# Conditioning rows loaded two weight tiles ahead of their sums, a row every six weight tiles, and the square of a relu on ScalarE

## The chip, the cores and the metric

The kernel runs on one core of a Trainium2 chip. A core has a matrix engine (TensorE, PE in the profile), three engines for elementwise work (VectorE or DVE, ScalarE or ACT, GpSimd or POOL) and an engine, SyncE (SP), that here only issues DMA transfers. Each engine runs its own instructions in the order in which they were put, and waits on semaphores for the others. The metric is the device time of one execution in microseconds, and lower is better.

## The reference

Two blocks of transformer layers run one after the other on 256 tokens of width 1024, all in fp32. The first block has two layers with three kinds of attention and an MLP with a squared relu. The second has two layers whose norms and outputs are conditioned on a vector: the `adaln` product gives a shift, a scale and a gate, for the tokens and for a context of 256 more.

```
def hybrid_layer(x, norm_mix, w_in, ..., w_o, norm_mlp, w_up, w_down, pos):
...
    return x + jnp.square(jax.nn.relu(h @ w_up)) @ w_down

def adaln(cond, w, b):
    m = jnp.matmul(jax.nn.silu(cond), w) + b
    return jnp.split(m, 3, axis=-1)

def modulated_norm(x, g, shift, scale):
    return rms_norm(x, g) * (1 + scale) + shift

def second_block(x, c, ctx, c_ctx, ...):
    for layer in range(DEPTH):
        shift, scale, gate = adaln(c, w_ada[layer], b_ada[layer])
        c_shift, c_scale, c_gate = adaln(c_ctx, w_ada[layer], b_ada[layer])
...
        x = x + gate[:, None] * jnp.matmul(y, w_out[layer])
        if need_ctx:
            x_ctx = x_ctx + c_gate * jnp.matmul(y_ctx, w_out[layer])
```

The `adaln` products do not depend on `x`, so the kernel may compute them at any time before block 2 uses them.

## The kernel before

The activations lie with the features on the partitions, in eight chunks of 128 x 256 tokens (`x0` to `x7`, which the order of the instructions below calls `x_92` to `x_99`). All matrix products are made of weight tiles of 128 x 1024 fp32 (512 KB). `weights()` loads one from HBM on SP's queue into one of six `raw` buffers (L284), lets ScalarE round it to a high part `hi` (L293) and VectorE subtract that from it to get the low part `lo` (L294; a few on POOL). There are three buffers each for `hi` and `lo`. TensorE then makes three matmuls for each product, `hi`·`h`, `hi`·`h`'s low part and `lo`·`h` (L336 to L338), 24 for a weight tile. The activations are split in the same way (`h` on L497 and L498, `ul`, `el` and others on L278).

The order on each engine is not written out. The kernel is a program of tiles, and a scheduler sets the order of the instructions from the order of the calls, its own model of the time and the free buffers.

After each attention, `wo` tiles project out, and each of the eight chunks of `x` is updated (L757 in block 1, L1168 for block 2's `wo2`); the squares of the new `x` are summed for the next norm: ScalarE squares (L421), POOL adds (L425), and TensorE makes the mean with an extra matmul (`ps_n`, L430). Then comes the MLP: 16 pairs of `wu` tiles, each ending in a relu on ScalarE (L774), its square (L775) and the split, and `wd` tiles, whose sums update `x` (L789, L790).

The conditioning product is made by VectorE. `wada` is laid out so that 48 tiles of 128 x 1024, here called rows, hold what 128 outputs of `adaln` need. A dot (L859) multiplies such a tile with the conditioning vector `crow` of the tokens or of the context and sums along it; the last eight rows need one dot only, so that there are 88. A generator (`Ada.rows`) goes one step forward on each fourth weight tile (`Ada.call`, at the end of `weights()`). `until(24)`, ahead of block 2, and `until(48)`, ahead of the norm of its second layer, run what is left of the rows that they need.

Of the kernel before, what the change touches and what calls it, by code (L numbers as in the profile page):

```python
# [12 lines left out]
AF = mybir.ActivationFunctionType  # L13
# [199 lines left out]
class _K:  # L213
# [4 lines left out]
    def __init__(self, tc, ctx, ins):  # L218
        self.tc, self.nc, self.ins = tc, tc.nc, ins
        pool = lambda n, **kw: ctx.enter_context(tc.tile_pool(name=n, bufs=1, **kw))  # L220
        self.res, self.wp, self.up, self.tp = pool("res"), pool("w"), pool("u"), pool("t")
        self.ps = pool("ps", space=PSUM)
        self.log_table, self.tanhs = None, []

        self.pending, self.rate = [], 1

        self.flows, self.tail = [], None

        self.rows = None
# [259 lines left out]
def block1(k, x, first, layers=(0, 1), fill=None):  # L489
    nc, ins = k.nc, k.ins  # L490
    g1 = k.g1

    def gx(c, gi):

        g = g1[:, gi * 8 + c:gi * 8 + c + 1]
        hi, lo = k.pair("h")
        nc.scalar.activation(hi, x[c], AF.Copy, scale=g)  # L497
        nc.vector.scalar_tensor_tensor(lo, x[c], g, hi, op0=ALU.mult, op1=ALU.subtract)  # L498
        return hi, lo
# [7 lines left out]
    for l in layers:  # L507
# [253 lines left out]
        for hf in range(2):  # L761
            u = []
            for b in range(8 * hf, 8 * hf + 8):
                p = k.psum()
                for f in range(2):
                    k.fm(p[:, f * T:(f + 1) * T], k.weights(ins["wu"][l, 2 * b + f]), 0, h)
                if rs2 is None:
                    rs2 = k.rstd(acc)
                    nc.vector.tensor_mul(rs2, rs2, rs2)
                    acc = k.acc()  # L770
                if fill:
                    fill(l, 1)
                r, uh, ul = k.t2("r"), k.u("uh", F32R, "v"), k.u("ul", F32R, "v")
                nc.scalar.activation(r, p, AF.Relu)  # L774
                nc.vector.tensor_mul(r, r, r)  # L775
                k.split(uh, ul, r)
                for f in range(2):
                    s = slice(f * T, (f + 1) * T)
                    u.append((uh[:, s], ul[:, s]))
            if hf:  # L780
                h = []
                if l == layers[-1]:
                    acc2 = k.acc()
            for c in range(NCH):
                p = k.psum()
                for q in range(2):
                    k.fm(p[:, :T], k.weights(ins["wd"][l, 2 * hf + q, c]), 0, u[8 * q:8 * q + 8], q == 0, q == 1)
                t = k.t1("dn")
                nc.vector.tensor_mul(t, p[:, :T], rs2)  # L789
                nc.vector.tensor_add(x[c], x[c], t)  # L790
                if fill:
                    fill(l, 1)
                if hf:
                    if l != layers[-1]:
                        h.append(gx(c, 2 * l + 2))
                    acc.add(c, x[c])
                    if l == layers[-1]:
                        acc2.add(c, x[c], g1[:, 32 + c:33 + c])
# [31 lines left out]
class Ada:  # L830

    EVERY = 4

    def __init__(self, k, cd):
        self.k, nc, ins = k, k.nc, k.ins
        sc, e = (k.res.tile([P, 2, NCH], F32, name=n) for n in ("sc", "sce"))
# [14 lines left out]
    def rows(self):  # L853
        k, nc = self.k, self.k.nc
        for l, i in ADA_ORDER:
            raw = k.raw(k.ins["wada"][l, i])
            for j in range(1 if (l, i // 8) == (1, 2) else 2):
                junk = k.tp.tile([P, D], mybir.dt.bfloat16, name="dot", tag="dot", bufs=1)
                nc.vector.tensor_tensor_reduce(out=junk, in0=raw, in1=self.c[:, j], scale=1.0, scalar=self.b[:, l, i:i + 1],  # L859
                                               op0=ALU.mult, op1=ALU.add, accum_out=k.ada[:, l, i, j:j + 1])  # L860
                yield
            self.done += 1
            if i == 15:
                v = k.ada[:, l, 8:16, :]
                nc.vector.tensor_scalar(v, v, 1.0, None, op0=ALU.add)
                nc.vector.tensor_tensor(v, v, k.g2[:, 8 * l:8 * l + 8, None].to_broadcast([P, 8, 2]), op=ALU.mult)

    def call(self):
        self.calls += 1
        if self.calls % self.EVERY == 0:  # L870
            next(self.steps, None)

    def until(self, n):
# [538 lines left out]
def _program(tc, ins, out, stop=7):  # L1412
    nc = tc.nc
    with ExitStack() as ctx:
# [68 lines left out]
        if stop & 3:  # L1483
            finish = block1(k, x, first, [l for l in range(2) if stop >> l & 1], fill if stop & 4 else None)
# [27 lines left out]
```

## Time and profile before

| | |
|---|---|
| time, median of 3 runs | 1436.06 us (1435.83 to 1436.11) |
| the profiled execution | 1436.98 us, of which the span of the trace is 1435.2 us |
| granted TensorE clock | 0.998 of full speed |
| TensorE (PE) busy | 1406.4 us, 98% |
| VectorE (DVE) busy | 1146.4 us, 80% |
| ScalarE (ACT) busy | 771.4 us, 54% |
| GpSimd (POOL) busy | 101.4 us, 7% |
| DMA engines busy | 49.3% for the weight queue |

Busy times are of one profiled execution. A matmul's duration overlaps with the next one's, so a busy TensorE is not a TensorE at its peak. In the timelines a row has the start in us from the beginning of the span, the duration, the engine, the line, the operation and its tiles, and in brackets how long the engine stood idle before it and what it waited for. Block 1 lasts until about 940 us.

### The profile page before, as it was taken

The page shows a single profiled execution, that of the slowest core. Times are in us where ns is not written, and L with a number is a line of the kernel's source. Part 1 is how long each engine was busy: PE and PEld are TensorE (multiplying, and loading weights), DVE is VectorE, ACT ScalarE, POOL GpSimd, SP SyncE. Part 2 cuts the span into 40 slices and gives each one's busy share as a digit, 9 for nine tenths or more (in the row PEclk, how much of TensorE's full clock was granted, in tenths as well). Part 3 has the DMA queues.
Part 4 walks back from the last instruction along what each step waited for, and adds up shares of the span by engine and source line. Part 5 has one row for each costly group of instructions (what it writes and reads, how often), then busy time and mean ns, then how long its engine had stood idle before and what let it go on. Part 6 is the DMA issues. An engine that isn't in the chain of part 4 may idle for free. (4 is left out here: it accounts for less than half of the span.)

```text
span 1435.2 us, 26253 instructions
## 1 busy us (share of the span) xinstructions
PE 1406.4 (98%) x10324; PEld 1281.4 (89%) x10324; DVE 1146.4 (80%) x2044; ACT 771.4 (54%) x1395; POOL 101.4 (7%) x84
## 2 busy tenths in 40 slices
PE   8999999999999999999999999989999999999999
PEld 7989999999999888899998999977677888987798
DVE  6887778998789887777888778788769979986776
ACT  5455665553455445556465455556653344656664
POOL 2000000100012200000011200310001002100000
PEclk9999999999999999999999999999999999999999
DMA  7734655665766563556575657642132128421223
GB/s 273 229 115 155 189 174 183 217 207 193 234 209 201 188 206 116 159 178 191 168 224 196 213 199 234 206 147 96 45 108 100 58 103 293 169 89 45 74 89 103
DMA packets 74279, 235.97 MB, mean 164 GB/s; under 512 B 9163, under 2 KB 11820, under 8 KB 74028
## 3 DMA queue, kind: packets, MB, share of 16 engines
q1 hardware_dynamic: 72284, 232.70, 49.3%
q8 instruction: 81, 1.33, 0.4%
q10 hardware_dynamic: 1872, 1.59, 0.3%
q14 instruction: 42, 0.34, 0.1%
HBM read 230.59 MB, written 3.68 MB: 163 GB/s over the span
## 5 line engine op out<-in xcount | busy, mean ns | idle before, releaser
L293 ACT CAST hi<-raw 128x1024 fp32r<-128x1024 f32 (+2 forms) x378 | 380.1, 1009 | 364.7 <-PE ps_mm L337 221.9
L294 DVE TENSOR_TENSOR lo<-raw,hi 128x1024 fp32r<-128x1024 f32 (+2 forms) x367 | 432.6, 1181 | 139.8 <-ACT hi L293 137.4
L336 PE MATMUL ps_mm<-h,hi 128*128 128x256 f32 (+1 forms) x1712 | 521.1, 305 | 2.2 <-ACT hi L293 0.8
L338 PE MATMUL ps_mm<-h,lo 128*128 128x256 f32 (+1 forms) x1712 | 511.5, 299 | 3.9 <-DVE lo L294 3.9
L337 PE MATMUL ps_mm<-h,hi 128*128 128x256 f32 (+1 forms) x1712 | 509.9, 298 | 1.2 <-DVE h L498 1.0
L336 PEld LDWEIGHTS ps_mm<-h,hi 128*128 128x128 f32 x1712 | 327.4, 191 | 29.9 <-issue 18.5
L338 PEld LDWEIGHTS ps_mm<-h,lo 128*128 128x128 f32 x1712 | 327.5, 191 | 16.5 <-DVE lo L294 5.2
L337 PEld LDWEIGHTS ps_mm<-h,hi 128*128 128x128 f32 x1712 | 327.6, 191 | 12.7 <-DVE h L498 2.8
L336 PE MATMUL ps_mm<-uh,hi 128*128 128x256 f32 x512 | 145.2, 284 | 0.0
L337 PE MATMUL ps_mm<-ul,hi 128*128 128x256 f32 x512 | 145.1, 283 | 0.1
L338 PE MATMUL ps_mm<-uh,lo 128*128 128x256 f32 x512 | 144.6, 283 | 0.0
L859 DVE CUSTOM_DVE_ANT_0 dot<-raw,crow,bada 128x1024 bf16<-128x1024 f32 x88 | 116.7, 1327 | 12.2 <-DMA raw<-wada 11.8
L425 POOL TENSOR_TENSOR acc<-acc,sq 128x256 f32<-128x256 f32 x54 | 52.3, 973 | 710.9 <-ACT sq L421 710.2
L336 PEld LDWEIGHTS ps_mm<-uh,hi 128*128 128x128 f32 x512 | 98.1, 192 | 2.6 <-issue 2.1
L337 PEld LDWEIGHTS ps_mm<-ul,hi 128*128 128x128 f32 x512 | 98.2, 192 | 1.0 <-DVE ul L278 0.5
L338 PEld LDWEIGHTS ps_mm<-uh,lo 128*128 128x128 f32 x512 | 98.1, 192 | 0.0
L336 PE MATMUL ps_mm<-hi,h 128*128 128x384 f32 (+1 forms) x192 | 62.6, 326 | 0.0
L337 PE MATMUL ps_mm<-lo,h 128*128 128x384 f32 (+1 forms) x192 | 61.3, 319 | 0.2 <-DVE lo L294 0.2
L338 PE MATMUL ps_mm<-hi,h 128*128 128x384 f32 (+1 forms) x192 | 61.2, 319 | 0.0
L336 PE MATMUL ps_mm<-y,hi 128*128 128x256 f32 x192 | 55.0, 288 | 0.0
L338 PE MATMUL ps_mm<-y,lo 128*128 128x256 f32 x192 | 54.9, 287 | 0.0
L337 PE MATMUL ps_mm<-y,hi 128*128 128x256 f32 x192 | 54.6, 285 | 0.0
(331 smaller groups left out, 2351.6 us busy)
## 6 DMA issues: line engine op xcount, KB each, us to landing
raw<-wu SPq DMA_DIRECT2D x64, 512.0 KB, 4.2
raw<-wd SPq DMA_DIRECT2D x64, 512.0 KB, 3.9
raw<-wada SPq DMA_DIRECT2D x48, 512.0 KB, 3.5
raw<-wg SPq DMA_DIRECT2D x48, 512.0 KB, 3.9
raw<-wo SPq DMA_DIRECT2D x48, 512.0 KB, 4.0
raw<-wqk SPq DMA_DIRECT2D x46, 512.0 KB, 4.5
raw<-w2e SPq DMA_DIRECT2D x32, 512.0 KB, 3.5
raw<-wv SPq DMA_DIRECT2D x32, 384.0 KB, 3.5
```

Of the source, the lines that this page charges most:

```text
L293: self.nc.scalar.copy(hi[:, s], raw[:, s])
L294: (self.nc.gpsimd if pool else self.nc.vector).tensor_sub(lo[:, s], raw[:, s], hi[:, s])
L336: mm(out, wh, xh, start=start, stop=False)
L337: mm(out, wh, xl, start=False, stop=False)
L338: mm(out, wl, xh, start=False, stop=stop)
L425: nc.gpsimd.tensor_add(self.sum, self.sum, sq)
L859: nc.vector.tensor_tensor_reduce(out=junk, in0=raw, in1=self.c[:, j], scale=1.0, scalar=self.b[:, l, i:i + 1], op0=ALU.mult, op1=ALU.add, ...
```

## The change

The generator now yields twice between a row's load and its first dot, and once after each dot as before. `call` steps it forward on four weight tiles of each six. The square of the relu is an activation on ScalarE in place of a product on VectorE.

```
                 nc.scalar.activation(r, p, AF.Relu)
-                nc.vector.tensor_mul(r, r, r)
+                nc.scalar.activation(r, r, AF.Square)
                 k.split(uh, ul, r)
...
-    EVERY = 4
-
...
         for l, i in ADA_ORDER:
             raw = k.raw(k.ins["wada"][l, i])
+            yield
+            yield
             for j in range(1 if (l, i // 8) == (1, 2) else 2):
...
     def call(self):
+
         self.calls += 1
-        if self.calls % self.EVERY == 0:
+        if self.calls % 6 < 4:
             next(self.steps, None)
```

Three places show how the instructions move. The first is VectorE at the last updates of `x` ahead of the MLP of block 1's first layer (`x_97` to `x_99` are the chunks 5 to 7, `h` the low part of the MLP's input, L859 a dot and the reading of its sum). Before:

```order
L498 SCALAR_TENSOR_TENSOR h<-x_97,g_90,h 128x256
L757 TENSOR_TENSOR x_98<-ps_mm,x_98 128x256
L294 TENSOR_TENSOR lo<-raw,hi 128x1024
L498 SCALAR_TENSOR_TENSOR h<-x_98,g_90,h 128x256
L757 TENSOR_TENSOR x_99<-ps_mm,x_99 128x256
L294 TENSOR_TENSOR lo<-raw,hi 128x1024
L498 SCALAR_TENSOR_TENSOR h<-x_99,g_90,h 128x256
L294 TENSOR_TENSOR lo<-raw,hi 128x1024
```

and in the changed kernel:

```order
L498 SCALAR_TENSOR_TENSOR h<-x_97,g_90,h 128x256
L859 ISA dot,adaT<-raw,crow,bada 128x1024
L859 ISA adaT 128x1
L757 TENSOR_TENSOR x_98<-ps_mm,x_98 128x256
L294 TENSOR_TENSOR lo<-raw,hi 128x1024
L498 SCALAR_TENSOR_TENSOR h<-x_98,g_90,h 128x256
L757 TENSOR_TENSOR x_99<-ps_mm,x_99 128x256
L859 ISA dot,adaT<-raw,crow,bada 128x1024
L859 ISA adaT 128x1
L498 SCALAR_TENSOR_TENSOR h<-x_99,g_90,h 128x256
L294 TENSOR_TENSOR lo<-raw,hi 128x1024 x3
```

Two dots now stand between the updates, and one of the `lo` tiles has moved behind the last `h`.

The second is VectorE at the end of block 2's first output projection, with the updates of `x_98` and `x_99` (chunks 6 and 7; L1168 is L1169 in the changed kernel) and the norm behind them (`nt`). Before:

```order
L859 ISA dot,adaT<-raw,crow,bada 128x1024
L859 ISA adaT 128x1
L1168 SCALAR_TENSOR_TENSOR x_98<-ps_mm,adaT,x_98 128x256
L859 ISA dot,adaT<-raw,crow,bada 128x1024
L859 ISA adaT 128x1
L859 ISA dot,adaT<-raw,crow,bada 128x1024
L859 ISA adaT 128x1
L1168 SCALAR_TENSOR_TENSOR x_99<-ps_mm,adaT,x_99 128x256
L294 TENSOR_TENSOR lo<-raw,hi 128x1024 x3
L376 SCALAR_TENSOR_TENSOR nt<-ps_n,rstd 128x256
L377 SCALAR_TENSOR_TENSOR nt<-nt,rstd 128x256
```

and in the changed kernel, from the update of chunk 5:

```order
L1169 SCALAR_TENSOR_TENSOR x_97<-ps_mm,adaT,x_97 128x256
L294 TENSOR_TENSOR lo<-raw,hi 128x1024
L1169 SCALAR_TENSOR_TENSOR x_98<-ps_mm,adaT,x_98 128x256
L294 TENSOR_TENSOR lo<-raw,hi 128x1024
L1169 SCALAR_TENSOR_TENSOR x_99<-ps_mm,adaT,x_99 128x256
L294 TENSOR_TENSOR lo<-raw,hi 128x1024
L376 SCALAR_TENSOR_TENSOR nt<-ps_n,rstd 128x256
L377 SCALAR_TENSOR_TENSOR nt<-nt,rstd 128x256
```

The dots are gone, and a `lo` tile follows each update.

The third is VectorE at the end of block 1's first MLP and the start of the second layer: the last `x` (`x_99`), its `h`, the first projection's `sh` and the norm `nt`. Before:

```order
L790 TENSOR_TENSOR x_99<-x_99,dn 128x256
L294 TENSOR_TENSOR lo<-raw,hi 128x1024
L498 SCALAR_TENSOR_TENSOR h<-x_99,g_90,h 128x256
L294 TENSOR_TENSOR lo<-raw,hi 128x1024
L542 STREAM_SHUFFLE sh<-ps_mm 128x512
L294 TENSOR_TENSOR lo<-raw,hi 128x1024
L859 ISA dot,adaT<-raw,crow,bada 128x1024
L859 ISA adaT 128x1
L859 ISA dot,adaT<-raw,crow,bada 128x1024
L859 ISA adaT 128x1
L294 TENSOR_TENSOR lo<-raw,hi 128x1024
L376 SCALAR_TENSOR_TENSOR nt<-ps_n,rstd 128x256
```

and in the changed kernel:

```order
L859 ISA dot,adaT<-raw,crow,bada 128x1024
L859 ISA adaT 128x1
L789 TENSOR_TENSOR dn<-ps_mm,rstd 128x256
L294 TENSOR_TENSOR lo<-raw,hi 128x1024
L790 TENSOR_TENSOR x_99<-x_99,dn 128x256
L859 ISA dot,adaT<-raw,crow,bada 128x1024
L859 ISA adaT 128x1
L498 SCALAR_TENSOR_TENSOR h<-x_99,g_90,h 128x256
L294 TENSOR_TENSOR lo<-raw,hi 128x1024
L542 STREAM_SHUFFLE sh<-ps_mm 128x512
L294 TENSOR_TENSOR lo<-raw,hi 128x1024 x2
L376 SCALAR_TENSOR_TENSOR nt<-ps_n,rstd 128x256
```

The two dots that stood ahead of the norm now stand around the last update of `x`, and one `lo` has moved ahead of that update.

## Rows read from the trace of the kernel before

**Rows 1.** The page, part 1: busy us of each engine, share of the span, instructions.
```profile
PE 1406.4 (98%) x10324; PEld 1281.4 (89%) x10324; DVE 1146.4 (80%) x2044; ACT 771.4 (54%) x1395; POOL 101.4 (7%) x84
```

**Rows 2.** Table of windows: busy time of each engine in two stretches.
```profile
core 0: us, PE busy (x) PEld busy (x) DVE busy (x) ACT busy (x) POOL busy (x), PEclk, DMA share, GB/s
1184.00:1212.00 28.00, 25.17 (x193) 24.28 (x193) 27.00 (x38) 13.97 (x21) 6.74 (x6) 0.96 0.85 291
...
300.00:460.00 160.00, 159.95 (x1276) 154.07 (x1275) 132.21 (x192) 77.56 (x98) 12.22 (x9) 1.00 0.64 208
```

**Rows 3.** The page, part 5: the dots; busy, mean ns, idle before, releaser.
```profile
L859 DVE CUSTOM_DVE_ANT_0 dot<-raw,crow,bada 128x1024 bf16<-128x1024 f32 x88 | 116.7, 1327 | 12.2 <-DMA raw<-wada 11.8
```

**Rows 4.** Table of waits: us in total, times, longest.
```profile
DVE dot L859 <- DMA raw<-wada: 11.8, 14, 2.1
```

**Rows 5.** Table of windows for the tile dot alone: first window.
```profile
0.00:920.00 920.00, 91.09 (x70) 1.00 0.60 194
```

**Rows 6.** Timeline of TensorE at 1205: start, duration, operation, [idle before, releaser].
```profile
1205.51 0.28 PE L338 MATMUL ps_mm<-y,lo 128*128 128x256 f32 x1
...
1207.79 0.70 PE L430 MATMUL ps_n<-acc,im 128*128 128x256 f32 x2 [2.00 <-POOL acc L425]
...
1209.79 1.22 PE L430 MATMUL ps_n<-sq,im 128*128 128x256 f32 x2 [0.83 <-ACT sq L421]
...
1212.94 0.34 PE L336 MATMUL ps_mm<-y,hi 128*128 128x256 f32 x1
```

**Rows 7.** Timeline of VectorE at 1200 to 1210.
```profile
1200.52 1.76 DVE L859 CUSTOM_DVE_ANT_0 dot<-raw,crow,bada 128x1024 bf16<-128x1024 f32 x1
...
1208.75 0.47 DVE L1168 SCALAR_TENSOR_TENSOR x<-ps_mm,adaT,x 128x256 f32<-128x256 f32 x1
1209.15 1.21 DVE L294 TENSOR_TENSOR lo<-raw,hi 128x1024 fp32r<-128x1024 f32 x1
```

**Rows 8.** Timeline of POOL (GpSimd) at 1200.
```profile
1200.11 1.07 POOL L425 TENSOR_TENSOR acc<-acc,sq 128x256 f32<-128x256 f32 x1 [2.15 <-ACT sq L421]
```

**Rows 9.** Timeline of TensorE: eight instructions behind a wait.
```profile
473.78 0.39 PE L337 MATMUL ps_mm<-h,hi 128*128 128x256 f32 x1 [0.33 <-DVE h L498]
...
487.38 0.27 PE L434 MATMUL ps_n<-im,acc 128*128 128x2 f32 x1 [0.73 <-DVE nt L376]
...
491.91 0.35 PE L336 MATMUL ps_mm<-h,hi 128*128 128x256 f32 x1 [0.62 <-DVE ntok L377]
...
531.54 0.48 PE L594 MATMUL ps_s<-qk 64*128 64x256 f32 x1 [0.76 <-DVE mn L599]
...
535.75 0.48 PE L594 MATMUL ps_s<-qk 64*128 64x256 f32 x1 [0.62 <-DVE mn L599]
...
957.98 1.12 PE L1050 MATMUL ps_n<-qsq,bo 128*128 128x512 f32 x2 [1.95 <-DVE qn L376]
...
961.98 1.12 PE L1050 MATMUL ps_n<-qsq,bo 128*128 128x512 f32 x2 [1.70 <-DVE qr L1054]
...
1080.31 0.50 PE L337 MATMUL ps_s<-el,fwh 128*128 128x512 f32 x1 [1.38 <-DVE el L278]
```

**Rows 10.** Timeline of VectorE at the places ahead of such waits.
```profile
276.49 0.47 DVE L498 SCALAR_TENSOR_TENSOR h<-x,g,h 128x256 fp32r<-128x256 f32 x1
...
483.24 1.29 DVE L859 CUSTOM_DVE_ANT_0 dot<-raw,crow,bada 128x1024 bf16<-128x1024 f32 x1 [1.09 <-DMA raw<-wada]
...
528.58 1.28 DVE L859 CUSTOM_DVE_ANT_0 dot<-raw,crow,bada 128x1024 bf16<-128x1024 f32 x1 [2.10 <-DMA raw<-wada]
...
954.78 1.27 DVE L859 CUSTOM_DVE_ANT_0 dot<-raw,crow,bada 128x1024 bf16<-128x1024 f32 x1
...
1075.02 1.28 DVE L859 CUSTOM_DVE_ANT_0 dot<-raw,crow,bada 128x1024 bf16<-128x1024 f32 x1 [1.88 <-DMA raw<-wada]
```

**Rows 11.** The tile r: relu and square; min/median/max ns.
```profile
L774 ACT ACTIVATE r<-ps_mm x32: 578/590/597, 281.7 to 889.9; 128x512 f32<-128x512 f32 x32
L775 DVE TENSOR_TENSOR r<-r x32: 676/682/689, 285.4 to 891.1; 128x512 f32<-128x512 f32 x32
```

More of the change, by code (lines that the diff above doesn't have):

```diff
@@ L774, in block1 @@
                 nc.scalar.activation(r, p, AF.Relu)
-                nc.vector.tensor_mul(r, r, r)
+                nc.scalar.activation(r, r, AF.Square)
                 k.split(uh, ul, r)
@@ L830 @@
 class Ada:
-    EVERY = 4
     def __init__(self, k, cd):
@@ L856, in rows @@
             raw = k.raw(k.ins["wada"][l, i])
+            yield
+            yield
             for j in range(1 if (l, i // 8) == (1, 2) else 2):
@@ L869, in call @@
         self.calls += 1
-        if self.calls % self.EVERY == 0:
+        if self.calls % 6 < 4:
             next(self.steps, None)
```

## The prediction

> **What bounds the kernel now.** I read the engines' busy time first. TensorE is busy for 1406.4 of 1435.2 us [rows 1], so all its idle time together is 28.8 us. No change in who waits for whom can bring much more than that, and no edit here takes a matmul away. So I looked for the stretches where TensorE loses time. The table of windows shows two kinds. From 300 to 460 us, in the middle of an MLP, TensorE is busy for 159.95 of 160 us (1276 matmuls, 0.125 us each), and VectorE for 132.21: there VectorE has 27.8 us to spare, and what it does costs nothing. From 1184 to 1212 us, at block 2's first output projection, it is the other way round: VectorE 27.00 of 28, TensorE 25.17 [rows 2]. The question is therefore where VectorE's order puts work ahead of something that TensorE waits for.
>
> The conditioning rows' dots are 88 instructions of 1327 ns, 116.7 us in all [rows 3]. VectorE also stands idle ahead of 14 of them, 11.8 us together, until the row's `wada` load has landed [rows 4]; since its instructions run in order, all that follows waits too. 70 of the 88 start before 920 us [rows 5], the other 18 in block 2. By the text of the change a row goes from eight weight tiles to six (to four and a half where it has one dot): 40 × 6 + 8 × 4.5 = 276 weight tiles for all rows, where it was 40 × 8 + 8 × 4 = 352. In the order of the changed kernel the last dot stands ahead of the end of block 1's last MLP, and block 2 has none. So each dot is either gone from where it was, or new somewhere earlier, and I priced the places one by one.
>
> **What the change takes away.**
>
> *The burst at 1188 to 1209 us.* The last eight dots stand between the eight updates of `x` (L1168). TensorE ends a matmul at 1205.51 + 0.28, waits 2.00 for POOL's sum of squares, then 0.83 for the last square, and is back at its usual work at 1212.94 [rows 6]. Between 1205.51 and 1212.94 lie 15 matmuls of 0.125 us and four passes of the mean (L430), which I put at 0.22 each (0.70 is shown for two that overlap): 1.9 + 0.9 = 2.8 of 7.4 us. So 4.6 are lost. The last `x` is updated at 1208.75, right behind two dots, and the `lo` of the next weight tile follows at 1209.15 [rows 7]; only then can the last square and the third matmul of each sum come. Without dots, the last update can follow its projection's last matmul at 1205.8, its square about 1 us later, and the new order has two `lo`s in hand by then. I take 4.5 of the 4.6, with 3 to 4.7 as bounds.
>
> The dot at 1200.52 took 1.76 us where one elsewhere takes 1.27 [rows 7, 10]; POOL's add of 1.07 us had begun at 1200.11 [rows 8] and ends where 0.5 us of the dot are explained. On this the Trainium skill, "SBUF — State Buffer" (SBUF: two separate sides), says that a VectorE instruction with two SBUF inputs and a GpSimd one share a port pair under an exclusive lock, so that the later one stands still until the earlier ends. The trace agrees (1.76 against 1.27). By that rule a dot beside an add would cost 0.5 us more wherever it is put.
>
> *Start of block 2, 954 to 962 us.* Two dots stand in the chain of the first key norm: one at 954.78, ahead of `qn` at about 957.5, the other ahead of `qr`. TensorE waits 1.95 and 1.70 there [rows 9, 10]. Without the first, `qn` comes 1.2 earlier; the second wait goes wholly. That is 2.9 at most. The scheduler has also reordered this attention, so I take 2.5 (0.5 to 2.9).
>
> *1075 to 1080 us.* VectorE waits 1.88 for `wada` and then makes two dots, ahead of the `lo` half of the hyena input (`el`); TensorE waits 1.38 for it [rows 9, 10]. The 1.88 + 2 × 1.28 = 4.4 us of delay vanish: 1.4 (1.0 to 1.5).
>
> *Layer 1 of block 1, 483 to 536 us.* At 483.24 a dot has waited 1.09 for its row, and a second one follows, ahead of a `lo` and the norm: TensorE waits 0.73 at 487.38, and 0.62 at 491.91. At 528.58 a dot has waited 2.10, ahead of the attention's scores (0.76 at 531.54), and another delays the second group (0.62 at 535.75) [rows 9, 10]. In the new order the first pair is gone, the pair at 528 is still there but without the wait for its load, and the last dot is gone. I take 0.7 + 0.5 + 0.6 + 0.6 = 2.4 (1 to 2.7).
>
> *The other six dots of block 2* (18 less the burst's eight, less two each at 954 and 1075) lie between waits of other causes; by the smallest wait above, 0.6, for one or two of them: 1.0 (0 to 2).
>
> Sum of the gains: 4.5 + 2.5 + 1.4 + 2.4 + 1.0 = 11.8.
>
> **What it adds.** 18 more dots now run before 920 us. Most fall in MLPs, where the spare 27.8 us of a 160 us stretch hide them [rows 2]. Were that cover gone, each would cost 1.28. Five places have none.
>
> *Start of both MLPs.* In layer 0 `h` of `x7` is made at 276.49 and `lo` tiles stand between the updates [rows 10]. Now two dots stand there, and one `lo` moves behind the last `h`. One more instruction of 1.2 in the chain makes `h` late by 1.2, and the displaced `lo` (needed at once by the next weight tile) ends some 0.5 late on top: 1.7. In layer 1 one dot stood there and now three do, with the same shift: 1.7. Together 3.4 (1.5 to 5; with POOL's adds beside each dot it is nearer the upper end).
>
> *End of layer 0's MLP.* TensorE waits 0.33 at 473.78 for the last `h` [rows 9]. Two dots now stand ahead of it; in the new order TensorE has 17 matmuls of a later tile (2.1 us) to make meanwhile, against 2.5 us of dots and a `lo` moved ahead: 0.6 (0 to 1.5).
>
> *The first 80 us and block 1's attention.* Two and about eight more dots; in the first, SP's queue also waits for the conditioning vector ahead of a weight load. Where I compared the orders, none stands right ahead of a norm or a score at which the old had none: 0.5 each (0 to 1, 0 to 1.5).
>
> *Loads.* A row holds one of six raw buffers for five tiles of six instead of four of eight. The weights lost a buffer of lead then too, and the table of waits names no wait for a load of `wu` or `wd`. Nothing.
>
> *The square on ScalarE.* r·r took 682 ns on VectorE; the relu of the same shape takes 590 on ScalarE [rows 11], so I price Square at 590 too (bounds 0.4 to 0.7). In 160 us of MLP ScalarE is busy for 77.56 [rows 2]; the 32 squares add 32 × 0.59 = 19 us over both layers, and VectorE is spared 32 × 0.682 = 21.8. TensorE is full on either side and the chain relu, square, cast, `ul` ends 0.1 us sooner. Nothing either way (−1 to +1).
> The Trainium skill, "ScalarE: Activation LUTs" (Rules for kernel authors), advises against this: simple functions such as `mul` belong on VectorE, not ScalarE. The trace differs for this fp32 shape: 682 on VectorE against 590 on ScalarE. By the rule the edit would lose time (rival 4); by the rows it is neutral.
>
> Sum of the costs: 3.4 + 0.6 + 0.5 + 0.5 = 5.0. Net 6.8 us. The profiled execution took 1436.98 us beside a median of 1436.06; its 1435.2 us of span become 1428.4, and the median 1436.1 − 6.8 = 1429.3.
>
> **The rivals.** What a measurement can tell from no change is 0.2%, 2.9 us: faster is below 1433.2, slower above 1438.9.
> 1. *Only the burst pays.* The rest of block 2 waits for something else next (the scheduler moved matmuls too), and layer 1 keeps its waits, while the costs come: 1436.1 − 4.5 − 1.4 + 5.0 = 1435.2, or 1432.7 if half of the costs do. For it: the waits of 0.6 to 0.8 have other instructions close behind. Against: two of them have an idle VectorE right ahead, waiting for `wada` [rows 10].
> 2. *The earlier dots cost more than the late ones did (slower).* The mechanism is one dot, 1.28 us (1.76 beside POOL), ahead of a norm, score or `h` in block 1. 18 of them come to 23 us. It decides from 11.8 + 2.9 = 14.7 us, 11 or 12 of the 18 uncovered: 1440. For it: five already are, by the order. Against: the cover in the MLPs [rows 2].
> 3. *Gain without the costs.* The `h` chain at the MLP starts has slack that the rows hide: 1436.1 − 11.8 = 1424.3.
> 4. *ScalarE's square binds.* Each half of an MLP ends its up projections with a square that may queue behind a relu and a cast of its own shape and so come 2 × 0.59 later than VectorE's did, with the sum for `wd` waiting; four halves, 4.7 us: 1429.3 + 4.7 = 1434. For it: nothing in the rows. Against: ScalarE's idle half [rows 2]. The page "ScalarE: Activation LUTs" of the Trainium skill, cited above, stands on this rival's side.
> 5. *The rows are not done in time* and block 2 makes a burst again: no change, 1436. Against: the order has no dot there.
>
> **How the numbers follow.** Forecast 0.56, its own range 1425.5 to 1432.5; rival 1 0.17; rival 2 0.08; rival 3 0.10; rival 4 0.05; rival 5 0.04. Faster are the forecast, rival 3 and half of rival 1 (0.74, with a little of rival 4, 0.76); same are the other half of rival 1, most of rival 4 and rival 5 (0.16); slower is 0.08. To leave no more than 2 in 10 out, the range reaches from just under rival 3 to rival 1's upper end: 1423 to 1435.5.
>
> **What the new profile would show.** VectorE's busy share from 1184 to 1212 falls from 27.00 by about 12 us and TensorE's waits of 2.00 and 0.83 are gone (step 1). No dot starts after about 890 us. VectorE's wait for `wada` falls from 11.8 to near nothing. Waits of 0.6 and more at 487, 531, 535, 958, 962 and 1080 are gone or below 0.3. TensorE's wait for `h` of `x7` at the MLP starts grows from some 0.2 to over 1. No wait names the Square. I would be wrong if the MLP starts cost over 3 us each, if the qk norm of block 2 waits for ScalarE instead, or if weight loads come late beside the rows.

## The result and the profile after

The changed kernel took 1447.1 us (median of 4 runs, 1444.92 to 1449.52), the kernel before 1436.09 (1435.83 to 1437.76): a ratio of 1.007, with a 95% interval of 1.0058 to 1.0083. It is 11 us slower, where 7 us less had been forecast. The profiled execution took 1447.96 us, with a span of 1446.2.

First the page, part 1, as in [rows 1], then the table of waits, as in [rows 4]:

```profile
PE 1414.5 (98%) x10324; PEld 1287.8 (89%) x10324; DVE 1127.4 (78%) x2012; ACT 790.0 (55%) x1427; POOL 102.9 (7%) x84
```

```profile
DVE dot L859 <- DMA raw<-wada: 29.6, 26, 3.0
```

VectorE has 19 us less to do, ScalarE 19 us more: the square has moved. TensorE is busy for 8 us longer with the same 10324 matmuls, so some of them ran slower. And VectorE's wait for the rows' loads, which an earlier load should have taken away, went from 11.8 to 29.6 us.

Where the time came and went can be read by following the same weight tiles in both traces. For each stretch of the kernel before (us of its trace), the fence has what the changed kernel took more or less, from the end of the last matmul of a weight tile at the stretch's end; beside it the kernels of the experiments that matter for it.

```
stretch of before    until 273  273-290  290-465  465-483  483-511  511-613  613-735  735-755  755-935  935-1182  1182-1214  1214-1398   sum
changed kernel          +3.3     +5.2     -0.3     +5.6     -1.4     +5.7     +0.1     +3.9     -0.3     -5.3       -4.8       -0.7     +11.0
e3_pace_only            -0.2     +3.8     +0.0     +0.6     -1.4     -1.5     -0.5     +1.2     +0.1     -5.0       -4.8       -0.7      -8.4
e7_shifted_by_two       -0.7     +1.2     -0.0     +0.6     -1.4     -1.6     -1.2     +1.8     +3.8     -5.2       -4.8       -0.6      -8.0
e8_pace_shifted_back    +6.6     +0.6     +0.8     +3.9     -1.4     -0.2     +0.8     +1.1     +5.5     -3.4       -4.8       -0.7      +8.8
e10_change_shifted      -1.5     +1.2     -0.3     +0.5     -1.4     -1.7     -1.2     +1.8     -0.3     -5.4       -4.8       -0.4     -13.5
e11_one_place           +3.3     +5.5     -0.3     +1.6     -1.4     +4.7     -0.1     +3.4     -0.2     -4.0       -4.8       -0.7      +6.9
e12_mlp_starts          +2.5     +0.0     -0.2     +6.0     -1.4     +1.4     +0.1     +0.9     -0.1     -3.7       -4.8       -0.7      +0.1
e13_attention_place     +1.7     +5.0     -0.0     +7.5     -1.4     -1.0     +0.2     +2.1     -0.3     -5.4       -4.8       -0.7      +2.9
e14_three_places        +2.5     -0.0     -0.2     +1.7     -1.4     -0.6     +0.1     +0.9     -0.3     -5.3       -4.8       -0.6      -8.2
```

Each row is one execution, and not all are typical: e11's was the longest of its ten (1443.91 us, median 1439.13), those of e8, e10 and e14 the shortest of theirs (1445.82, 1423.45 and 1428.79, medians 1450.65, 1426.38 and 1431.19).

Block 2 gave back 10.8 us, where the prediction's terms for it come to 9.4. Block 1 cost 21.8, mostly in four stretches: the two MLP starts (273 to 290, 735 to 755), the end of layer 0's MLP (465 to 483) and layer 1's attention (511 to 613), with 3.3 more in the first 273 us, which no run here was made to explain.

In block 2 the burst is gone. The tables of windows for the tile dot, as in [rows 5], and for the first output projection, as in [rows 2]:

```profile
0.00:920.00 920.00, 113.50 (x88) 0.99 0.60 197
```

```profile
1199.00:1227.00 28.00, 28.00 (x228) 27.47 (x227) 18.46 (x27) 15.99 (x24) 8.16 (x6) 1.00 0.60 204
```

All 88 dots stand ahead of 920 us, and at the projection TensorE now has no idle time in 28 us, where it had 25.17 busy.

In block 1 the longest new stall is at the end of layer 0's MLP. First SyncE's timeline (the issue of the load), then VectorE's, as in [rows 10], and TensorE's, as in [rows 9]:

```profile
478.92 0.33 SPq L284 DMA_DIRECT2D raw<-wada  x1
```

```profile
480.30 1.21 DVE L294 TENSOR_TENSOR lo<-raw,hi 128x1024 fp32r<-128x1024 f32 x1
483.27 1.28 DVE L859 CUSTOM_DVE_ANT_0 dot<-raw,crow,bada 128x1024 bf16<-128x1024 f32 x1 [1.76 <-DMA raw<-wada]
484.48 0.08 DVE L859 DVE_READ_ACCUMULATOR2_ANT adaT<- 128x1 f32 x1
484.48 0.42 DVE L789 TENSOR_TENSOR dn<-ps_mm,rstd 128x256 f32<-128x256 f32 x1
484.82 1.21 DVE L294 TENSOR_TENSOR lo<-raw,hi 128x1024 fp32r<-128x1024 f32 x1
485.95 0.42 DVE L790 TENSOR_TENSOR x<-x,dn 128x256 f32<-128x256 f32 x1
486.28 1.28 DVE L859 CUSTOM_DVE_ANT_0 dot<-raw,crow,bada 128x1024 bf16<-128x1024 f32 x1
487.49 0.08 DVE L859 DVE_READ_ACCUMULATOR2_ANT adaT<- 128x1 f32 x1
487.49 0.48 DVE L498 SCALAR_TENSOR_TENSOR h<-x,g,h 128x256 fp32r<-128x256 f32 x1
```

```profile
486.09 0.39 PE L338 MATMUL ps_mm<-h,lo 128*128 128x256 f32 x1 [3.42 <-DVE lo L294]
486.31 0.38 PE L336 MATMUL ps_mm<-h,hi 128*128 128x256 f32 x1
```

The row's load was issued at 478.92. VectorE came to its dot at 481.5 and stood still until 483.27. The end of the MLP (`dn`, `x`) and the `lo` of the next weight tile were ready for it and had to wait behind the dot; a second dot stands between the last `x` and its `h`. So a dot's own 1.28 us became 1.76 + 1.28 ahead of the `lo`, and TensorE waited 3.42 us.

Then comes what made each of these stalls dearer. Tables of windows behind three of them (columns as in [rows 2]; the column before the last two is the granted clock):

```profile
283.00:288.00 5.00, 5.00 (x25) 5.00 (x25) 1.82 (x2) 1.04 (x1) 0.00 (x0) 0.50 0.77 239
...
485.00:490.00 5.00, 3.91 (x20) 3.92 (x21) 2.97 (x5) 0.85 (x3) 0.00 (x0) 0.66 0.55 183
490.00:495.00 5.00, 5.00 (x44) 5.00 (x43) 2.09 (x4) 3.02 (x3) 1.03 (x1) 1.00 1.00 365
...
550.00:555.00 5.00, 5.00 (x17) 3.48 (x17) 3.11 (x9) 3.26 (x9) 0.00 (x0) 0.50 0.27 85
```

A granted clock of 0.50 is the lower of TensorE's two levels, 1.2 of 2.4 GHz. From 283 to 288 us it made 25 matmuls in 5 us and was never idle; from 490 to 495, at full clock, 44. Behind these stalls the engine went on at half speed for some us. Over block 1, matmuls that ran longer cost more than the waiting itself. TensorE alone (us, busy, clock, DMA share, GB/s), first block 1 of the kernel before, then of the changed kernel:

```profile
0.00:935.00 935.00, 921.64 (x7197) 1.00 0.60 195
```

```profile
0.00:956.80 956.80, 933.86 (x7197) 0.99 0.60 197
```

TensorE's idle time went from 13.4 to 22.9 us, 9.6 more, and the same 7197 matmuls took 12.2 us longer: together the 21.8.

Of the Trainium skill's two statements that the prediction used, the one on `mul` ("ScalarE: Activation LUTs", Rules for kernel authors) was not borne out for this fp32 shape (e1, below). The tile r, as in [rows 11]:

```profile
L774 ACT ACTIVATE r<-ps_mm x32: 583/592/598, 289.3 to 911.9; 128x512 f32<-128x512 f32 x32
L775 ACT ACTIVATE r<-r x32: 619/632/634, 290.1 to 912.5; 128x512 f32<-128x512 f32 x32
```

The square took 632 ns on ScalarE, 0.04 more than I priced and 0.05 less than it took on VectorE.

### The profile page after: what moved, and what is told of

Read it like the earlier page. It is cut to its first block, busy times and chain, and to the rows that moved or that the text cites. A ratio compares the mean times of both kernels' runs of the same rounds, so it can differ in the third digit from the quotient of the medians.

```text
span 1446.2 us, 26254 instructions
## 1 busy us (share of the span) xinstructions
PE 1414.5 (98%) x10324; PEld 1287.8 (89%) x10324; DVE 1127.4 (78%) x2012; ACT 790.0 (55%) x1427; POOL 102.9 (7%) x84
## 5 line engine op out<-in xcount | busy, mean ns | idle before, releaser
L336 PEld LDWEIGHTS ps_mm<-h,hi 128*128 128x128 f32 x1712 | 330.6, 193 | 31.0 <-issue 12.9
L338 PEld LDWEIGHTS ps_mm<-h,lo 128*128 128x128 f32 x1712 | 330.9, 193 | 21.2 <-DVE lo L294 10.9
L337 PEld LDWEIGHTS ps_mm<-h,hi 128*128 128x128 f32 x1712 | 331.1, 193 | 14.5 <-DVE h L498 4.7
L859 DVE CUSTOM_DVE_ANT_0 dot<-raw,crow,bada 128x1024 bf16<-128x1024 f32 x88 | 113.5, 1290 | 29.8 <-DMA raw<-wada 29.6
L425 POOL TENSOR_TENSOR acc<-acc,sq 128x256 f32<-128x256 f32 x54 | 56.1, 1042 | 712.5 <-ACT sq L421 709.7
```

What stands on the lines that cost most here:

```text
L336: mm(out, wh, xh, start=start, stop=False)
L337: mm(out, wh, xl, start=False, stop=False)
L338: mm(out, wl, xh, start=False, stop=stop)
L425: nc.gpsimd.tensor_add(self.sum, self.sum, sq)
```

## The experiments

The theories were these. **A**: the denser pace puts dots ahead of work that TensorE waits for, and long stalls also halve the clock. **B**: a load that stands ahead holds one of six raw buffers for longer, the rows' loads themselves come late, and that is the loss. **C**: the square on ScalarE. After the first four runs A became **D**: the two yields do not give the load a lead, they only move load and dots, together, to other places, and the places decide. Each ratio stands with its 95% interval against runs of the kernel before on the same chip.

**The change in its parts.** e1 is the kernel before with the square alone:

```
-                nc.vector.tensor_mul(r, r, r)
+                nc.scalar.activation(r, r, AF.Square)
```

> Only the square moves to ScalarE; the rows stay as they were. Theory A (dots of the denser pace stand ahead of work that TensorE waits for, and each long stall also halves the granted clock for some us) and theory B (the longer hold of a raw buffer delays the rows' own loads, and VectorE waits ahead of the dots): no difference, 1434 to 1437 us. Theory C (the square on ScalarE is what costs): 1440 us or more.

Measured: 1438.32 us, ratio 1.0006 (0.9993 to 1.0019). The time lies between the two ranges, and the interval holds 1: no difference is shown, and C falls.

e2 is the changed kernel with the square back on VectorE.

> The rows change as in the changed kernel; the square stays on VectorE. A and B: as slow as the changed kernel, 1444 to 1450 us, with the waits at the two MLP starts and at the end of layer 0's MLP. C: 1434 to 1440 us.

Measured: 1445.63 us, ratio 1.0066 (1.0050 to 1.0083). The rows are the whole loss. In its trace it does not lie wholly at the changed kernel's places: read as in the table, e2 lost 6.8 us in the first 273, 4.5 and 3.3 at the MLP starts, 6.1 at the end of layer 0's MLP, and nothing (−0.1) at 511 to 613.

e3 keeps the pace and drops the two yields; e4 keeps the yields and goes back to a row per eight tiles (both from e2):

```
 e3:
-            yield
-            yield
...
-        if self.calls % 6 < 4:
+        if self.calls % 3 == 0:
...
 e4:
-        if self.calls % 6 < 4:
+        if self.calls % 8 < 4:
```

> A row every six tiles, but no yields between its load and its first dot (load and dot 0, three tiles later dot 1); square on VectorE. A: the stalls at the MLP starts and at layer 1's start stay, 1440 to 1448 us, VectorE's wait for wada can be as small as before (about 12 us). B: the wait for wada falls under 15 us and with it the time, to 1428 to 1434 us.

> The load stands two tiles ahead of its first dot, but a row takes eight tiles as before, so the burst in block 2 stays; square on VectorE. A: near the kernel before, 1433 to 1440 us, no stall over 1.5 us at the MLP starts. B: the buffer is held seven tiles of eight, the wait for wada stays near 30 us and the time is 1440 us or more.

Measured: e3 1429.11 us, ratio 0.9952 (0.9936 to 0.9967); e4 1434.53, ratio 0.9984 (0.9971 to 0.9997). In e3 and e2 the dots are called at the same weight tiles; only the load is called two tiles earlier in e2, and that costs 16.5 us. A's forecast for e3 (1440 us or more) fell, and B's for e4. The time of e3 is B's, but not for B's reason: VectorE's wait for the rows in e3 and in e4:

```profile
DVE dot L857 <- DMA raw<-wada: 28.0, 25, 4.1
```

```profile
DVE dot L859 <- DMA raw<-wada: 20.7, 24, 2.9
```

e3 is the fast one and waits 28.0 us for its rows, 1 us away from e2's 26.9; e4, which by its calls holds a buffer for seven tiles of eight, loses nothing. What differs is the place. In e3's order no dot stands beside the last `x` of layer 0's MLP; in e2's and the changed kernel's two do. The scheduler had put the dots at much the same distance behind their load, whatever distance the calls give them: from the issue of a row's load to its first dot it was 4.15 us in the kernel before (median of 48), 4.34 in the changed kernel, 4.42 in e2 and 4.22 in e3. That it goes by its model of when the load lands is my reading; no run tests it. Nor was a buffer held much longer: from the issue to the end of a row's last dot it was 8.28 us in the kernel before, 8.74 in the changed kernel, 9.17 in e2 and 8.55 in e4 (medians).

**Moving the rows without changing them.** e5 lets dot 1 follow sooner; e7 is e2 begun two tiles later; e8 is e3 begun two tiles earlier, so that its loads are called where e2's are; e9 is e3's third phase:

```
 e5:
-        if self.calls % 6 < 4:
+        if 1 <= self.calls % 6 <= 4:
...
 e7:
-        if self.calls % 6 < 4:
+        if self.calls > 2 and (self.calls - 2) % 6 < 4:
...
 e8:
-        if self.calls % 3 == 0:
+        if self.calls % 3 == 1:
...
 e9:
-        if self.calls % 3 == 0:
+        if self.calls % 3 == 2:
```

> As e2 (row every six tiles, load two tiles ahead, loads at the same tiles), but dot 1 follows dot 0 after one tile, so a row's buffer is held three tiles of six, not five. Theory B (what costs is that the load stands ahead and holds a raw buffer): most of the loss goes, 1428 to 1437 us. Theory D (the yields don't bring the load closer to the dots' needs, they move load and dots together, and the loss is set by which places the dots fall on): in this order two dots still stand around the last x of layer 0's MLP and between the last updates ahead of both MLPs, so still 1440 to 1450 us.

> Exactly e2 (row every six tiles, load two tiles ahead, buffer held five of six), begun two weight tiles later. B: as slow as e2, 1442 to 1449 us. D: in this order the last x of layer 0's MLP and the last x ahead of both MLPs have no dot beside them, so 1427 to 1434 us.

> e3 (row every six tiles, load and dot 0 in one step) begun two tiles earlier, so that its loads stand at the same tiles as in e2, without yields between load and dot. B: as e3, 1427 to 1433 us. D: the dots fall on the same places as in e2 and the changed kernel, 1438 to 1449 us, with the long stall at layer 1's start.

> e3 with the third possible phase. B: as e3, 1427 to 1433 us. D: it differs from e3 by where its dots fall: one dot ahead of the last x of both MLP starts, none at layer 0's MLP end: 1427 to 1438 us.

Measured: e5 1442.15 us, ratio 1.0045 (1.0027 to 1.0062); e7 1427.06, 0.9939 (0.9920 to 0.9958); e8 1450.65, 1.0090 (1.0061 to 1.0118); e9 1436.44, 0.9986 (0.9973 to 1.0000). e7 and e8 part the theories: the same rows as in e2, with the same hold of the buffer, become 18.6 us faster when they begin two tiles later, and e3, which has no yields, becomes as slow as e2 when its loads stand where e2's stand (a little above D's range). e5 and e9 lie in D's ranges and outside B's. B falls.

D holds only in part, for the place alone does not set the price. From the end of layer 0's MLP to the last rows e8 has almost all its dots at the places where e2 has them, but in the table it lost only 1.1 us at layer 1's MLP start, where e2 lost 3.3; 6.6 of its loss lie in the first 273 us and 5.5 at 755 to 935, where its last rows stand elsewhere. At layer 1's attention the dots of row 28 stand at the same place of VectorE's order in e2, e8 and the changed kernel. This is the first of them in e2:

```profile
545.34 1.29 DVE L859 CUSTOM_DVE_ANT_0 dot<-raw,crow,bada 128x1024 bf16<-128x1024 f32 x1 [1.86 <-DMA raw<-wada]
```

It waited 1.86 us for its load in e2 and 1.57 in e8, and the stretch lost nothing (−0.1 and −0.2); in the changed kernel it waited 2.95, and the stretch lost 5.7. So by these traces a place's price depends also on how late the load lands there and on whether the clock falls behind the stall. TensorE's stall at layer 1's start in e8, and what stands there in e10 below:

```profile
484.34 0.58 PE L338 MATMUL ps_mm<-h,lo 128*128 128x256 f32 x1 [2.94 <-DVE lo L294]
```

**The places one by one.** e11, e12 and e13 are the changed kernel with one or two of the 48 rows begun two or three tiles later; in e12 the rows behind these two (15 and 39) also begin one tile later. e14 has all three edits:

```
 e11 (row 25):
-        if self.calls % 6 < 4:
+        if (self.calls % 6 < 4) != (self.calls in (145, 146, 148, 149)):
...
 e12 (rows 14 and 38):
-        if self.calls % 6 < 4:
+        if (self.calls % 6 < 4) != (self.calls in (79, 80, 81, 82, 83, 88, 223, 224, 225, 226, 227, 232)):
...
 e13 (row 28):
-        if self.calls % 6 < 4:
+        if (self.calls % 6 < 4) != (self.calls in (163, 164, 166, 167)):
```

> The changed kernel with one row alone (the 25th) begun two tiles later, so that its two dots stand behind the first norm input of layer 1 and not around the last x of layer 0's MLP; all other rows as in the changed kernel. D: the stall of 3.4 us there and the half clock behind it go, 6 to 8 us less than the changed kernel: 1439 to 1442 us. If the place is only a symptom and the delay comes back behind it: 1445 us or more.

> The changed kernel with two rows alone (the 14th and the 38th) begun three tiles later, so that no dot stands among the last updates of x ahead of either MLP. D: 5.2 and 3.9 us come back, less what these places cost in the kernel before: 1438 to 1442 us. By the price that the prediction gave these places (1.7 each): 1443 to 1445 us.

> The changed kernel with one row alone (the 28th) begun two tiles later, so that its dots, the first of which waited 2.95 us for its load, stand behind layer 1's first scores and not ahead of them. D: the stall of 2.8 us and the half clock from 547 to 556 us go, 4 to 7 us less than the changed kernel: 1440 to 1443 us. If the stall is not the dot's: 1446 us or more.

> The changed kernel with four of its 48 rows begun later (the 14th and 38th by three tiles, the 25th and 28th by two): e11, e12 and e13 at once. If the three places are the whole loss and independent: the single gains add up (1447.1 less some 7, 10 and 6), 1421 to 1427 us, as fast as the shifted change or faster. If a delay taken out at one place comes back at the next: 1430 to 1436 us.

Measured: e11 1439.13 us, ratio 1.0018 (1.0006 to 1.0030); e12 1436.83, 0.9992 (0.9979 to 1.0005); e13 1440.80, 1.0026 (1.0015 to 1.0037); e14 1431.19, 0.9961 (0.9947 to 0.9975). Against the changed kernel's ratio of 1.007 the single edits are worth 0.0052, 0.0078 and 0.0044, that is 7.5, 11.2 and 6.3 us, and all three 0.0109, 15.7 us. Each place is a cause: two dots of 1.28 us moved by two tiles are worth 6 to 8 us (e11, e13). e12 came out faster than D had it.

But the gains do not add up to e14's, which missed the time expected for independent places and lies in the range for delays that come back. In the stretches of its trace the delays did not come back: the three places are repaired (0.0, +1.7, −0.6 and +0.9 against +5.2, +5.6, +5.7 and +3.9), 18.4 of the 19.2 us between the two traces. What the single runs count twice is in part the attention: at 511 to 613 the changed kernel lost 5.7, e11 4.7 and e12 1.4, though neither of the last two moved a row there; row 28's first dot waited 2.95, 1.97 and 1.82 us. What the lower clock costs behind a stall differs too: with TensorE waiting 3.42 us at the end of layer 0's MLP in the changed kernel and 3.41 in e13, the stretch lost 5.6 and 7.5. And four runs of the changed kernel spread by 4.6 us. The rest of the difference I leave open.

**The whole change, begun two tiles later.** e10 is the changed kernel with e7's line, the square on ScalarE included.

> The whole change (rows and the square on ScalarE), its rows begun two weight tiles later. Theory D (the loss is set by which places the dots fall on): 1424 to 1431 us, as e7, since e1 showed the square to be worth nothing either way. Theory B: 1442 us or more. A theory in which square and rows disturb each other: over 1433 us.

Measured: 1426.38 us (5 runs, 1423.45 to 1426.89), ratio 0.9919 (0.9903 to 0.9936): by the ratio 11.6 us faster than the kernel before, and the lowest time here, though its interval overlaps e7's. Its page, part 1, then the end of layer 0's MLP in TensorE's timeline and in VectorE's, with the row's dot behind it:

```profile
PE 1402.2 (99%) x10324; PEld 1279.7 (90%) x10324; DVE 1127.4 (79%) x2012; ACT 790.9 (56%) x1427; POOL 101.3 (7%) x84
```

```profile
473.63 0.39 PE L337 MATMUL ps_mm<-h,hi 128*128 128x256 f32 x1 [0.48 <-DVE h L498]
```

```profile
471.62 0.42 DVE L790 TENSOR_TENSOR x<-x,dn 128x256 f32<-128x256 f32 x1
471.96 1.22 DVE L294 TENSOR_TENSOR lo<-raw,hi 128x1024 fp32r<-128x1024 f32 x1
473.10 0.48 DVE L498 SCALAR_TENSOR_TENSOR h<-x,g,h 128x256 fp32r<-128x256 f32 x1
...
481.14 1.28 DVE L859 CUSTOM_DVE_ANT_0 dot<-raw,crow,bada 128x1024 bf16<-128x1024 f32 x1 [3.33 <-DMA raw<-wada]
```

Here the same dot waits 3.33 us for its load, longer than in the changed kernel, and costs nothing: what TensorE needs is done ahead of it. The stall of 3.42 has become 0.48.

## Why the prediction was wrong

*What the change takes away* was right for block 2, in its mechanisms and close in size. The burst: 4.5 predicted, 4.8 measured, the same in every kernel without dots there. Block 2 ahead of it (954 to 962, 1075 and the other dots): 2.5 + 1.4 + 1.0 = 4.9 predicted, 5.3 measured. One of the two waits at 958 and 962 stayed, though, with 1.98 us for `qn`. The waits of 1.70 and 1.38 are gone, 3.1 us, and most of the other 2.2 came back between 1008 and 1032 us, where I had named no wait. In layer 1, the pair of dots at 483 to 487 is gone as forecast: 1.2 predicted, 1.4 measured at 483 to 511. The square was neutral, as predicted.

*What it adds* failed. For block 1 costs of 5.0 less a gain of 2.4 were predicted, and 21.8 net measured. One of the prediction's own signs of being wrong came true: both MLP starts cost over 3 us. Three steps were wrong.

The first is that an earlier load would be there when the dot comes. "The pair at 528 is still there but without the wait for its load" stands in the term for layer 1, and all other terms take a dot for 1.28 us. In the trace the first dot of that pair waited 2.95 us, TensorE then 2.81 behind it. The timeline of VectorE and of TensorE in the changed kernel:

```profile
541.53 1.29 DVE L859 CUSTOM_DVE_ANT_0 dot<-raw,crow,bada 128x1024 bf16<-128x1024 f32 x1 [2.95 <-DMA raw<-wada]
```

```profile
545.70 1.60 PE L594 MATMUL ps_s<-qk 64*128 64x256 f32 x8 [2.81 <-DVE mn L599]
```

At the MLP starts, too, the first dot waited, 0.86 and 1.06 us. I had read the order of VectorE after the change, where the dots' places stand, and not how far behind its load a dot would come: some 4.3 us, whatever distance the program gives the two. The premise of the term *Loads* falls with it: a row held its buffer for 8.74 us (median), about three weight tiles of 24 × 0.12 us, and not for five. The sentence "VectorE's wait for `wada` falls from 11.8 to near nothing" was the check for it and came out as 29.6.

The second is that a stall costs its length. The terms for the MLP starts (1.7 each) and for the end of layer 0's MLP (0.6) are lengths of waits. They were 5.2, 3.9 and 5.6. At the first of them two dots stand in VectorE's order, and TensorE waited 1.08, 0.37 and 0.53 us:

```profile
276.89 1.28 DVE L859 CUSTOM_DVE_ANT_0 dot<-raw,crow,bada 128x1024 bf16<-128x1024 f32 x1 [0.86 <-DMA raw<-wada]
...
280.78 1.27 DVE L859 CUSTOM_DVE_ANT_0 dot<-raw,crow,bada 128x1024 bf16<-128x1024 f32 x1
```

```profile
280.58 0.39 PE L337 MATMUL ps_mm<-h,hi 128*128 128x256 f32 x1 [1.08 <-DVE h L498]
...
281.46 0.53 PE L336 MATMUL ps_mm<-h,hi 128*128 128x256 f32 x1 [0.37 <-ACT h L497]
282.52 0.58 PE L337 MATMUL ps_mm<-h,hi 128*128 128x256 f32 x1 [0.53 <-DVE h L498]
```

2.0 us in all, and behind it 5 us at half clock, in which 25 matmuls were made instead of 44: 19 × 0.12 = 2.3 us more. The kernel before shows the same at the burst, and the prediction priced the burst without it: behind the waits of 2.00 and 0.83 the granted clock was 0.70 (TensorE alone).

```profile
1210.00:1215.00 5.00, 5.00 (x29) 0.70 0.94 276
```

The third is the cover at the end of layer 0's MLP, where most of the cost is the wait of 3.42. The matmul at 486.09 (above) needs the `lo` that stands behind the first dot, and most of the 17 matmuls that I counted as cover stand behind it. I counted them without looking at what they wait for.

Rival 2 is what happened: the earlier dots cost more than the late ones did. It had 0.08. Its point of decision, 11 or 12 of 18 dots uncovered at 1.28 us each, was wrong, since with the wait for the load and the lower clock moving four rows, eight dots, by two or three tiles (and two more rows by one) was worth 15.7 us (e14).

## What to carry to other kernels

An instruction that is "moved ahead" in a program whose order a scheduler sets has only a new place, and it is the place that has to be priced: read in the order what stands right behind it on its engine, and add the wait for its operand to its own time. Side work with a fixed period lands on the few tight places by its phase; try the phases before judging the pace, since here one and the same change was 0.7% slower or 0.8% faster by where it began. And the price of a stall of a full matrix engine is its length and the half clock that may follow: at the first MLP start 2.0 us of waiting and 2.3 of slow matmuls.

## What the hardware showed that I had not expected

The clock fell behind some stalls and not behind others of the same length. Behind 2.81 us (545.70 in the changed kernel) the granted clock was 0.50 from 550 to 555. Behind 1.72 us at the same place in e2 it stayed at 1.00, behind 1.65 us at the end of layer 0's MLP in e4 too, and behind 1.68 us in e12, again at the changed kernel's place, it was 0.66 in the next window. The windows of e2, e4 and e12 behind these stalls (in the last the columns are TensorE alone, clock, DMA share, GB/s):

```profile
549.00:554.00 5.00, 4.49 (x25) 3.22 (x25) 4.68 (x16) 2.43 (x6) 0.00 (x0) 1.00 0.72 227
```

```profile
480.00:485.00 5.00, 5.00 (x44) 5.00 (x43) 2.81 (x4) 2.31 (x3) 1.74 (x1) 1.00 1.03 388
```

```profile
540.00:545.00 5.00, 5.00 (x22) 0.66 0.48 153
```

What decides between them no run here was made to tell.
